# Loading the first pair of a batched matmul in two halves per operand, with its own order of k

## The chip, the cores and the metric

The kernel runs on one core of a Trainium2 chip. The metric is the device time in microseconds (us), the median over several executions. The profile's span, from the first to the last instruction, is some 2 us shorter than that time: in the profiled run of the kernel before, 121.9 us against 123.82.

Words used below: the profile counts 16 DMA engines for the core. They move data between DRAM and the on-chip memory (SBUF; a cast here reads a tile of 128 partitions, 128x2048 in the profile). A kernel issues a DMA from a queue, here that of SyncE. An engine's share of a transfer comes as packets, whose times and sizes the trace has (but not which engine moved them). In this kernel TensorE multiplies (512 matmuls), VectorE casts (32 casts), ScalarE moves results out (32 copies).

## The reference

```python
batch, m, k, n = 16, 512, 512, 512
a: (batch, k, m) float32;  b: (batch, k, n) float32

def reference(a, b):
    return np.matmul(a.transpose(0, 2, 1), b).astype(np.float32)
```

Sixteen products of 512 x 512 matrices. In all 33.55 MB are read and 16.78 MB are written.

## The kernel before

Matrices are taken in pairs (G = 2). A pair of one operand is one load of 2 MB: partition (g, q) receives R = 8 consecutive rows of matrix g, 16 KB side by side. Four input buffers take a and b of two pairs. VectorE casts each buffer in two halves (v = 0, 1) to bf16, TensorE sums over k, ScalarE evicts, and all stores are issued after all loads.

```python
G = 2; Q = P // G      # 64 partitions for each matrix of the pair
R = K // Q; V = 2; RV = R // V
in_v = [x.rearrange("(pair g) (q r) m -> pair (g q) r m", g=G, r=R) for x in (a, b)]
out_v = out.rearrange("(pair g) (c t) n -> pair c g t n", g=G, t=T)
NX = 4
# ... (tiles and semaphores)
for n in range(2 * pairs):                      # SyncE: loads
    if n >= NX:
        nc.sync.wait_ge(s_in, n - NX + 1)       # a cast has freed the buffer
    nc.sync.dma_start(x_ts[n % NX][:], in_v[n % 2][n // 2]).then_inc(s_x[n % NX], 16)
for i in range(pairs - 1):                      # SyncE: stores
    nc.sync.wait_ge(s_out, i + 1)
    nc.sync.dma_start(out_v[i], o_ts[i % NO][:]).then_inc(s_o if i else s_o0, 16)

for i in range(pairs):                          # VectorE: casts
    for v in range(V):
        # ... (waits for TensorE)
        for n in (2 * i, 2 * i + 1):
            if v == 0:
                nc.vector.wait_ge(s_x[n % NX], 16 * (n // NX + 1))
            nc.vector.tensor_copy(out=(bbf_ts if n % 2 else abf_ts)[v][:],
                                  in_=x_ts[n % NX][:, v * RV:(v + 1) * RV, :]).then_inc(s_cast, 1)
            # ... (after v == 1: s_in + 1)
```

The sum over k may be taken in any order, so long as a and b agree. That is why a pair may have its own assignment of rows to partitions.

## Time and profile before

| | before |
|---|---|
| time, median of 6 runs | 124.0 us (123.82 to 124.23) |
| span of the profiled run | 121.9 us |
| mean DMA rate, share of 16 engines' time | 413 GB/s, 97.6% |
| TensorE / VectorE / ScalarE busy | 51% / 31% / 26% |
| first cast of a, of b | 8.84 us, 13.67 us |
| last computing ends | 92.6 us |

The profile's slices are 40 equal parts of the span, each digit the busy share in tenths. The prediction below shows them, the waits and the start.

### The profile page before, as it was taken

How to read it: one execution, taken by the hardware profiler on the slowest of the kernel's cores; microseconds unless marked ns; L12 is line 12 of the kernel's file. 1: busy time of each engine (PE TensorE's matmuls, PEld its weight loads, DVE VectorE, ACT ScalarE, POOL GpSimd, SP SyncE). 2: the span in 40 equal slices, each digit the busy share in tenths (PEclk: the TensorE clock that was granted, in tenths of full speed). 3: DMA queues.
4: the chain of work that ended last, by engine and by line, in shares of the span. 5: the costliest groups of instructions: out<-in, count | busy, mean ns of one | idle time of the engine just before them, and what ended most of it. 6: DMA issues, size and time to landing. Idle time of an engine off the chain costs nothing. (4 is left out here: it accounts for less than half of the span.)

```text
span 121.9 us, 1261 instructions
## 1 busy us (share of the span) xinstructions
PE 62.5 (51%) x512; PEld 35.8 (29%) x512; DVE 38.0 (31%) x48; ACT 31.8 (26%) x41; POOL 0.2 (0%) x4
## 2 busy tenths in 40 slices
PE   0000099989669749969919988946960000000000
PEld 0000044546246314536605645624630000000000
DVE  0003560784194092474356247419000000000000
ACT  4000000480920830190470075091083000000000
POOL 0000000000000000000000000000000000000000
PEclk9999999999999977999995899999999655555555
DMA  5899999999999999999999999999999999999994
GB/s 108 360 430 430 436 430 430 430 430 430 430 430 430 430 430 436 430 430 430 430 430 430 430 430 430 436 390 428 428 430 430 430 428 430 430 430 428 428 428 175
DMA packets 4480, 50.33 MB, mean 413 GB/s; under 512 B 384, under 2 KB 384, under 8 KB 384
## 3 DMA queue, kind: packets, MB, share of 16 engines
q1 hardware_dynamic: 4480, 50.33, 97.6%
HBM read 33.55 MB, written 16.78 MB: 413 GB/s over the span
## 5 line engine op out<-in xcount | busy, mean ns | idle before, releaser
L103 PE MATMUL ps<-bbf,abf 64*128 64x512 bf16 x512 | 62.5, 403 | 27.9 <-PEq L98 27.9
L103 PEld LDWEIGHTS ps<-bbf,abf 64*128 64x128 bf16 x512 | 35.8, 114 | 54.1 <-issue 37.8
L121 ACT COPY o<-ps 128x1024 f32<-128x1024 f32 x32 | 30.1, 1026 | 59.8 <-PE ps L103 59.8
L82 DVE CAST abf<-x 128x2048 bf16<-128x2048 f32 x16 | 19.6, 1224 | 26.6 <-PE ps L103 17.6
L82 DVE CAST bbf<-x 128x2048 bf16<-128x2048 f32 x16 | 19.6, 1225 | 20.8 <-DMA x<-in_b_dram 20.8
L126 ACT ACTIVATE done<-done 1x1 uint32<-1x1 uint32 x8 | 1.6, 196 | 0.0
L121 ACT ACT_TABLE_LOAD x1 | 1.3, 1283 | 0.9 <-SPq L64 0.9
L88 DVE MEMSET done<- 1x1 f32 x16 | 0.9, 59 | 0.0
L148 POOL MEMSET const-bfloat16-1.0<- 128x1 bf16 x1 | 0.1, 101 | 0.0
L148 POOL MEMSET const-uint8-127<- 128x1 uint8 x1 | 0.1, 101 | 0.0
L148 POOL MEMSET const-float32-0.0<- 128x1 f32 x1 | 0.1, 98 | 0.2 <-issue 0.2
L148 POOL MEMSET const-float32-1.0<- 128x1 f32 x1 | 0.1, 98 | 0.0
## 6 DMA issues: line engine op xcount, KB each, us to landing
x<-in_a_dram SPq DMA_DIRECT2D x8, 2048.0 KB, 12.1
x<-in_b_dram SPq DMA_DIRECT2D x8, 2048.0 KB, 15.9
out_dram<-o SPq DMA_DIRECT2D x8, 2048.0 KB, 30.8
```

Source lines behind the costliest of these rows:

```text
L82: nc.vector.tensor_copy(out=(bbf_ts if n % 2 else abf_ts)[v][:], in_=x_ts[n % NX][:, v * RV:(v + 1) * RV, :],).then_inc(s_cast, 1)
L88: nc.vector.memset(dve_done[:, n:n + 1], 0.0).then_inc(s_in, 1)
L103: mm = nc.tensor.matmul(ps_ts[g][h][:, t % 2, :], a_m[:, t], bbf_ts[v][rows, r, :], start=(v == 0 and r == 0), stop=(v == V - 1 and r == R ...
L121: ev = nc.scalar.copy(out=o_ts[i % NO][:, g, 2 * h:2 * h + 2, :], in_=ps_ts[g][h][:])
L126: nc.scalar.memzero(act_done[:, i:i + 1]).then_inc(s_out, 1)
L148: nc = _bacc.Bacc("TRN2", target_bir_lowering=False, num_devices=1)
```

## The change

Pair 0 alone is loaded in two DMAs per operand. Each takes half of the rows of both matrices (256 of 512), as 8 KB runs that lie side by side in DRAM. All other loads stay as they were. The apparent intent is a first half that is complete in itself; but the wait asks for both halves before the first cast, so no work can begin on one half.

```diff
+    in0_v = [
+        x[0:G].rearrange("g (v q r) m -> v g q r m", v=V, r=RV) for x in (a, b)
+    ]
...
-            nc.sync.dma_start(x_ts[n % NX][:], in_v[n % 2][n // 2]).then_inc(s_x[n % NX], 16)
+            if n < 2:
+                for v in range(V):
+                    nc.sync.dma_start(
+                        x_ts[n][:, v * RV:(v + 1) * RV, :], in0_v[n][v]
+                    ).then_inc(s_x[n], 16)
+            else:
+                nc.sync.dma_start(x_ts[n % NX][:], in_v[n % 2][n // 2]).then_inc(s_x[n % NX], 16)
...
-                        nc.vector.wait_ge(s_x[n % NX], 16 * (n // NX + 1))
+                        nc.vector.wait_ge(s_x[n % NX], 16 * (n // NX + 1 + (n % NX < 2)))
```

## The prediction

> **What bounds the kernel now.** I read the overview in slices first, because it says which resource never rests.
>
> ```profile
> PE   0000099989669749969919988946960000000000
> DVE  0003560784194092474356247419000000000000
> ACT  4000000480920830190470075091083000000000
> DMA  5899999999999999999999999999999999999994
> GB/s 108 360 430 430 436 430 430 430 430 430 430 430 430 430 430 436 430 430 430 430 430 430 430 430 430 436 390 428 428 430 430 430 428 430 430 430 428 428 428 175
> DMA packets 4480, 50.33 MB, mean 413 GB/s; under 512 B 384, under 2 KB 384, under 8 KB 384
> ...
> q1 hardware_dynamic: 4480, 50.33, 97.6%
> ```
>
> TensorE, VectorE and ScalarE all have gaps and are done by slice 32 of 40. The DMA row is at 9 from the third slice to the last but one, at 428 to 436 GB/s with one dip to 390. So the kernel is bound by its 50.33 MB of traffic: 50.33 MB at 430 GB/s is 117.0 us, and the rest of the 121.9 us span is the start and the end. The packet line says more: 24 DMAs were issued (16 loads, 8 stores), and there are 384 packets under 512 B, which is 24 x 16. Every DMA left 16 small packets, one for each of 16 engines: each transfer was spread over all of them. One engine's share of the steady rate is 430 / 16 = 26.9 GB/s.
>
> Next come the chain of work that ended last and the DMA queue's own waits, to see whether anything but traffic sets the end.
>
> ```profile
> 90.68 0.92 ACTq L64
> 91.60 0.92 ACT o L121
> 92.52 0.06 ACT done L126
> ```
>
> ```profile
> SPq L68 <- DVE done L88: 59.1, 12, 13.0
> SPq L159 <- DMA out_dram<-o: 27.8, 1, 27.8
> ```
>
> The last computing ends at 92.6 us; the 27.8 us behind it are spent waiting for stores that are queued. The 59.1 us that the queue waited for VectorE before reissuing a load cost nothing: earlier loads still filled the engines. Computing has some 29 us of slack at the end.
>
> Last, the timeline of the start, which is what the change touches.
>
> ```profile
> 0.94 0.39 SPq L68 DMA_DIRECT2D x<-in_a_dram  x1
> 1.39 0.42 SPq L68 DMA_DIRECT2D x<-in_b_dram  x1
> 1.86 0.42 SPq L68 DMA_DIRECT2D x<-in_a_dram  x1
> 2.32 0.69 SPq L68 DMA_DIRECT2D x<-in_b_dram  x1
> 8.84 1.23 DVE L82 CAST abf<-x 128x2048 bf16<-128x2048 f32 x1 [8.84 <-DMA x<-in_a_dram]
> 13.67 1.23 DVE L82 CAST bbf<-x 128x2048 bf16<-128x2048 f32 x1 [3.60 <-DMA x<-in_b_dram]
> ...
> 16.08 0.33 SPq L68 DMA_DIRECT2D x<-in_a_dram  x1
> ```
>
> The four first loads are issued within 3 us. Each operand of a pair is 2 MB; b of pair 0 lands 4.8 us after a, as 2.10 MB at 430 GB/s (4.9 us) says. The first reload is issued 2.4 us after b's first cast starts.
>
> [...] Both old access patterns have 128 outermost; for the store the author even put the 128 rows ahead of g. [...]
>
> **The change part by part.**
>
> *What it seems to offer, and doesn't.* Halves of 1 MB could let casting start earlier, but VectorE's wait for pair 0 now asks for 32 on each semaphore, so the first cast still waits for both halves. Nothing in computing starts earlier. The new order of k is the same for a and b and sums the same products. Casts, matmuls and evictions keep count and shape: zero.
>
> *Two more issues.* Each is 0.39 to 0.42 us on the queue that starts transfers. Pair 1's loads are issued some 0.9 us later, while earlier loads fill the engines: zero on the path.
>
> *Smaller packets.* Pair 0 now comes in 4 x 128 = 512 packets of 8 KB instead of 256 of 16 KB. The stores already move 8 KB runs, at 428 against 430 GB/s in the late slices. On 4.19 MB (9.75 us) that is under 0.1 us.
>
> *The new outermost dimension.* This is the expensive part. The old source view merges g and q: 128 rows, 16 KB apart. In the new one a half is (g, q, r, m) with v fixed: g steps by a whole matrix (1 MB), q by 8 KB, and 64 x 8 KB is only half a matrix, so g and q cannot merge. The slowest dimension on the DRAM side is g, of size 2; on the on-chip side it is 128 partitions. [...] I therefore expect each of the four new DMAs to run on **two engines, not sixteen**, and on the same two[...].
>
> The sum for one of these two engines:
> - Before, its share of pair 0 was 4.19 MB / 16 = 0.262 MB, at 26.9 GB/s 9.75 us.
> - After, it is 4.19 MB / 2 = 2.097 MB, 78.0 us.
> - All else, 14 loads and 8 stores, stays on 16 engines, so it also carries what it carried before.
> - Added: 78.0 - 9.75 = 68.2 us, in series on this engine.
>
> How much of that is on the path? All of it. In the kernel before each engine works without a break from about 2 us to the end (DMA at 9 in each slice), so two of them get 68.2 us more and nothing gets less on them. The other fourteen run dry, which helps nobody, because a later load is only complete when its shares on the two slow engines land. Nor do these two rest: pair 0 lands at about 2 + 78 = 80 us; then pair 1's shares follow (another 9.75 us, to about 90), and the first reload is issued some 2.4 us after pair 0's last cast can start, about 83 us, well before 90. From there the picture before repeats, moved by 68 us. Sum: 124.0 + 68.2 = 192.2 us; with 0.2 for 8 KB packets and longer start effects, **192.4 us**.
>
> **The rivals.**
> 1. *All 16 engines are used anyway* (the transfer is regrouped on its way to the engines[...]). For it: nothing in the kernel's code says two engines, and the stores have a dimension of 2 too. Against it: that 2 stands second, behind 128. The change would then only swap 16 KB for 8 KB packets in 4 of 50 MB: 123.7 to 124.4 us.
> 2. *Sixteen engines and a quicker start.* The second slice moves only 360 GB/s; smaller first packets could fill the pipeline sooner. At full rate from slice 1 the first two slices would move 860 against 468, so the most to win is (860 - 468) / 430 x 3.05 = 2.8 us, and much of that is the delay before the first issue at 0.94 us. I would give it 0.5 us: 123.5 us, still within 2%.
> 3. *Two engines, but more loss than the sum*: a gap between pair 1 and the first reload[...]. That issuing can block is visible: one store's issue took 9.07 us against 0.44 for the quickest. I expect pair 1's loads to be held back this way, but they sit behind pair 0 on the two engines in any case. It could add a few us: 195 to 200.
> 4. *Two engines that go faster with the others silent.* If memory, not the engine, set the 26.9 GB/s, two alone could do better. [...] The steady 430 in both directions speaks for a limit of the engines.
>
> **Range and chances.** Rivals 3 and 4 set the range around 192.4: 186 to 199. Rivals 1 and 2 together get 0.12[...]. Faster by over 2% (under 121.5) needs more than the start can give: 0.01. Slower: 0.87.
>
> **What would show it right or wrong.**
> - Small packets: 22 x 16 + 4 x 2 = 360 with two engines, 416 with sixteen. Data packets are 4352 in both.
> - GB/s near 2 x 26.9 = 54 in the slices before 80 us, apart from what pair 1's loads add on the others; about 430 in the later stretch, at least where all engines have work.
> - The queue's share of 16 engines' time down from 97.6% to about 62% (the same work over 190 us).
> - First cast of a near 41 us (half of 78, plus 2), of b near 80; first reload near 83.
> - The first computing at 80 and the last some 68 us later than before, near 161.
> - If the two first casts stay near 9 and 14 us, the engine count was the wrong step, and the time is 124. If b is cast at 80 but the end is far from 192, the step "nothing rests after that" was wrong.

The sum: 124.0 + 68.2 + 0.2 = 192.4 us, but the two engines in it stand there as an assumption; experiments 1 and 2 test it.

## The result, and the profile after

The changed kernel takes 200.11 us (199.56 to 200.53, 6 runs) against 124.0 us. The ratio is 1.613, with a 95% interval of 1.610 to 1.616. Ratios here are the mean time of one kernel's fast runs over that of the other's fast runs of the same rounds, so not quite the ratio of the medians.

The slices of the changed kernel, each 4.97 us long, and its packets:

```profile
PE   0000000000000000006998586977698776000000
DVE  0000000020000000007272727272726360000000
ACT  2000000000000000000075252255225616000000
...
DMA  0111111111129992114999999999999999999991
GB/s 20 53 53 56 53 53 53 54 54 53 53 89 241 292 238 74 53 56 122 419 383 347 426 389 436 442 422 413 436 422 434 419 426 426 426 429 431 427 416 51
DMA packets 4712, 50.33 MB, mean 253 GB/s; under 512 B 360, under 2 KB 360, under 8 KB 360
...
q1 hardware_dynamic: 4712, 50.33, 64.2%
```

For ten slices the core moves 53 GB/s, which is 2 of 16 engines (2 x 26.9 = 54), and the DMA row stands at 1 tenth (a share of 0.13 from 4 to 58 us, and 2/16 is 0.125). The small packets are 360 and not 416: 22 DMAs left 16 of them and four left 2. Then come three slices, 59.6 to 74.5 us, in which the DMA row is at 9 but only 238 to 292 GB/s move: the engines are occupied, yet slow. From slice 20 on the rate is mostly back above 410, as before.

The timeline of issues and casts of the changed kernel answers to the one of before in the prediction:

```profile
0.96 1.26 SPq L74 DMA_DIRECT2D x<-in_a_dram  x2
2.26 37.02 SPq L74 DMA_DIRECT2D x<-in_b_dram  x2
39.32 19.21 SPq L78 DMA_DIRECT2D x<-in_a_dram  x1
42.82 1.23 DVE L92 CAST abf<-x 128x2048 bf16<-128x2048 f32 x1 [42.82 <-DMA x<-in_a_dram]
58.57 2.11 SPq L78 DMA_DIRECT2D x<-in_b_dram  x1
89.47 1.23 DVE L92 CAST bbf<-x 128x2048 bf16<-128x2048 f32 x1 [45.42 <-DMA x<-in_b_dram]
...
91.88 0.33 SPq L78 DMA_DIRECT2D x<-in_a_dram  x1
```

The columns are start, duration, engine, line and what was done. Casts of pair 0 begin at 42.8 and 89.5 us instead of 8.8 and 13.7. Look also at the durations of issuing: b's two DMAs kept SyncE for 37 us and pair 1's first load for 19 us, against 0.4 to 0.7 us before. The first of pair 1's packets starts at 59.2 us, so the other 14 engines stood idle until then. Of pair 1's 256 packets of 16 KB, 224 (14 shares of 16) started from there to 76 us and the other 32 only from 87.9 us on, when the two engines were coming to the end of pair 0.

From the first cast of b to the end there are 121.9 - 13.67 = 108.2 us before and 198.6 - 89.47 = 109.1 us after. Nearly all of the loss lies ahead of that cast.

The rates of the changed kernel in stretches of its time show what happened after 59 us (the last two columns are the DMA share and GB/s; the first is the stretch):

```profile
4.00:58.00 54.00, 0.00 (x0) 0.00 (x0) 1.23 (x1) 0.00 (x0) 0.00 (x0) 1.00 0.13 53
59.00:64.00 5.00, 0.00 (x0) 0.00 (x0) 0.00 (x0) 0.00 (x0) 0.00 (x0) 1.00 1.01 242
64.00:66.00 2.00, 0.00 (x0) 0.00 (x0) 0.00 (x0) 0.00 (x0) 0.00 (x0) 1.00 1.01 365
66.00:76.00 10.00, 0.00 (x0) 0.00 (x0) 0.00 (x0) 0.00 (x0) 0.00 (x0) 1.00 0.95 229
77.00:88.00 11.00, 0.00 (x0) 0.00 (x0) 0.00 (x0) 0.00 (x0) 0.00 (x0) 1.00 0.13 54
```

Before 59 us and after 77 us two engines work alone at 53 to 54. Between, 16 engines work (share about 1), at little more than half of 430. The trace's own packet records say the same from the other side: an 8 KB packet of the two engines takes 0.309 us when they are alone and mostly 0.5 to 0.67 us here, and a 16 KB packet of the other fourteen mostly 1.0 to 1.25 us instead of 0.611. From 67 to 75 us none of 101 such packets took less than 0.99 us, so all fourteen were slow. This is the part that the prediction lacked. The stretch from 64 to 66 us is different: there 38 of 40 such packets took 0.66 to 0.81 us and only two 1.10 and 1.29; of nine 8 KB packets six took 0.33 to 0.41 us and three 0.58 to 0.67.

### The profile page after: what moved, and what is told of

Same layout as the page of the kernel before. It is cut to its first block, busy times and chain, and to the rows that moved or that the text cites. A ratio compares the mean times of both kernels' runs of the same rounds, so it can differ in the third digit from the quotient of the medians.

```text
span 198.6 us, 1263 instructions
## 1 busy us (share of the span) xinstructions
PE 62.7 (32%) x512; PEld 35.9 (18%) x512; DVE 38.0 (19%) x48; ACT 31.8 (16%) x41; POOL 0.2 (0%) x4
## 5 line engine op out<-in xcount | busy, mean ns | idle before, releaser
L92 DVE CAST abf<-x 128x2048 bf16<-128x2048 f32 x16 | 19.6, 1224 | 61.0 <-DMA x<-in_a_dram 42.8
```

## The experiments

Seven kernels were run. The first three ask why 16 engines became two and what it is that costs; the next two what the 8 us beyond the prediction are; the last two follow up a miss of mine.

### 1. Two DMAs per operand in the old order of k

```diff
-                        x_ts[n][:, v * RV:(v + 1) * RV, :], in0_v[n][v]
+                        x_ts[n][:, v * RV:(v + 1) * RV, :],
+                        in_v[n][0][:, v * RV:(v + 1) * RV, :],
```

The source's slowest dimension is again the 128 rows; the count of DMAs, their size and the 8 KB runs are those of the change.

> Pair 0 in the same four DMAs of 8 KB runs, but in the old order of k, so that the source's slowest dimension is 128 rows and not g = 2. Theory 'two engines': all 16 engines are used again, 416 packets under 512 B, first casts near 9 and 14 us, time 124.0 (123.6 to 124.6). Rival 'smaller packets or two more issues cost the time': clearly over 126, up to 200.

Measured: correct, 124.18 us (124.07 to 124.44), ratio 1.002 (0.9997 to 1.0037). The page of this run:

```profile
DMA  3999999999999999999999999989999999999993
GB/s 72 399 428 428 444 428 428 439 428 433 428 428 444 439 428 434 434 428 428 434 434 428 428 428 428 423 337 431 423 428 428 428 428 428 428 428 428 428 428 147
DMA packets 4768, 50.33 MB, mean 411 GB/s; under 512 B 416, under 2 KB 416, under 8 KB 416
```

There are 416 small packets, so 26 DMAs of 16 shares each, and casts at 8.58 and 13.47 us. Halving the loads, 8 KB packets and two more issues cost nothing that can be told from zero. The rival falls. What remains as the cause is the source's pattern, in which two things differ: the size of the outermost dimension, and runs that lie side by side. Experiment 2 separates them.

### 2. The new order of k, one DMA per half and per matrix

```diff
                 for v in range(V):
-                    nc.sync.dma_start(
-                        x_ts[n][:, v * RV:(v + 1) * RV, :], in0_v[n][v]
-                    ).then_inc(s_x[n], 16)
+                    for g in range(G):
+                        nc.sync.dma_start(
+                            x_ts[n][g * Q:(g + 1) * Q, v * RV:(v + 1) * RV, :], in0_v[n][v][g]
+                        ).then_inc(s_x[n], 16)
```

(The wait counts four DMAs per buffer.) The bytes go where the change puts them; only g is no longer a dimension of a DMA.

> The new order of k and the 8 KB runs side by side are kept, but each of the four DMAs is cut into one per g, 64 rows each, so that g is no dimension of a DMA any more. Theory 'two engines': 16 engines again, 480 packets under 512 B, time 124 to 134 (64 rows at a time may not keep all engines at full rate), guess 127. Rival 'runs that lie side by side in DRAM are slow to read, whatever engine reads them': pair 0 still lands near 80 to 90 us, time near 200.

Measured: correct, 132.57 us median, ratio of the fast runs 1.068 (1.066 to 1.071); one further run, at 140.32, was 6% above the others of this kernel and so is a slow one. With g gone from each DMA there are 480 small packets, so 16 engines again: runs that lie side by side don't confine these DMAs to two engines (16 small packets each), and the dimension of 2 in front did (2 each in the changed kernel). But my guess of 127, inside the stated 124 to 134, was 5.6 us too low:

```profile
DMA packets 4832, 50.33 MB, mean 386 GB/s; under 512 B 480, under 2 KB 480, under 8 KB 480
...
3.00:20.00 17.00, 0.00 (x0) 0.00 (x0) 1.23 (x1) 0.00 (x0) 0.00 (x0) 1.00 1.03 223
22.00:82.00 60.00, 45.76 (x386) 27.04 (x388) 29.97 (x38) 22.89 (x30) 0.00 (x0) 0.97 1.01 432
```

While pair 0 is loaded, all engines are busy (share 1.03) at 223 GB/s, half of the 432 of the later stretch. At 223 GB/s the pair's 4.19 MB take 18.8 us instead of 9.75, so 9.1 us more; the time rose by 8.6 us (132.57 against 123.95 for the kernel before beside it). Experiments 6 and 7 ask why.

### 3. Pair 1's loads held until pair 0 has landed

```diff
+            if n == 2:
+                nc.sync.wait_ge(s_x[1], 32)
```

> The changed kernel, but pair 1's two loads are issued only when pair 0 has landed whole. Theory 'contention': the 8 us by which the two engines ran late were lost beside pair 1's traffic on the other 14; without it pair 0 lands at 2.4 + 256 x 0.309 = 81.5 us (b cast near 82 instead of 89.5), about 2 us are then lost before pair 1 starts, and the time is about 195 (193 to 197). Rival 'the two engines slow down after 58 us by themselves': b cast still near 89 us, time 201 to 204.

Measured: correct, 195.42 us (195.24 to 195.79), ratio 1.576 (1.573 to 1.580). The timeline and the windows of this run:

```profile
43.04 1.23 DVE L94 CAST abf<-x 128x2048 bf16<-128x2048 f32 x1 [43.04 <-DMA x<-in_a_dram]
82.18 0.36 SPq L80 DMA_DIRECT2D x<-in_a_dram  x1
82.19 1.23 DVE L94 CAST bbf<-x 128x2048 bf16<-128x2048 f32 x1 [37.92 <-DMA x<-in_b_dram]
```

```profile
4.00:81.00 77.00, 0.00 (x0) 0.00 (x0) 1.23 (x1) 0.00 (x0) 0.00 (x0) 1.00 0.13 54
86.00:140.00 54.00, 45.21 (x358) 25.20 (x354) 25.00 (x31) 19.08 (x25) 0.00 (x0) 0.91 1.01 432
```

With nothing beside them, the two engines keep 54 GB/s to the end and b is cast at 82.19 us, 7.3 us sooner than in the changed kernel. So the two engines do not slow down by themselves: pair 1's loads beside them cost the 7.3 us. From this cast to the end it is 193.3 - 82.2 = 111.1 us, 2.9 us more than before the change: pair 1's first packet starts only at 83.2 us, and no packet starts from 82 to 83. The cast of b (expected near 82) and the time (193 to 197) are both as expected.

### 4. Only a in the new way

```diff
-            if n < 2:
+            if n < 1:
...
-   16 * (n // NX + 1 + (n % NX < 2))
+   16 * (n // NX + 1 + (n % NX < 1))
```

> Only a of pair 0 comes in the new way, b in one DMA as before (the orders of k then differ, so pair 0's result is wrong on purpose). Theory 'two engines, and contention per load that passes on the other 14': half the extra work, 128 x 0.309 - 4.9 = 34.7 us, so 159 without contention; three loads pass instead of two, at about 3.8 us each, so about 168 (164 to 172). Rival 'the loss beside the two engines is a single fixed cost': 159 + 8 = 167 cannot be told from it, but 159 to 161 would deny contention.

Measured: 168.7 us (168.69 and 168.72), ratio 1.360 (1.357 to 1.364); the result is wrong, for the two operands' orders of k differ in pair 0. Half of the extra work on two engines accounts for 159 us; the rest, 9.7 us, is what three passing loads cost, after the 7.3 us that two cost in experiment 3. The loss beside the two engines is there again, so the case of no contention (159 to 161) is refuted. Whether it is a cost per load stays undecided: 9.7 lies between the 7.3 of a single fixed cost and the 11.0 of three loads at the 3.65 us each of experiment 3. (The expectation's own sum was off: 159 and three times 3.8 is 170.4, not 168.) The windows of this run show something else:

```profile
23.00:26.00 3.00, 0.00 (x0) 0.00 (x0) 0.00 (x0) 0.00 (x0) 0.00 (x0) 1.00 0.98 336
27.00:35.00 8.00, 0.00 (x0) 0.00 (x0) 0.00 (x0) 0.00 (x0) 0.00 (x0) 1.00 1.00 229
36.00:40.00 4.00, 0.00 (x0) 0.00 (x0) 0.00 (x0) 0.00 (x0) 0.00 (x0) 1.00 1.01 233
40.40:42.40 2.00, 0.00 (x0) 0.00 (x0) 0.00 (x0) 0.00 (x0) 0.00 (x0) 1.00 1.03 356
```

The slowness is not even. By the count of 8 KB packets in the trace, the two engines were at the first eight of the 64 rows of their half from 23.2 to 26.6 us, and reached the 32nd row at 40.4 us. In both stretches the rate is far higher than between. Where they are makes a difference; but a row stands for a place on chip and for a place in DRAM at once.

### 5. The same with the source moved by 64 KB

```diff
-        x[0:G].rearrange("g (v q r) m -> v g q r m", v=V, r=RV) for x in (a, b)
+        x.rearrange("b k m -> (b k) m")[32:32 + G * K].rearrange(
+            "(g v q r) m -> v g q r m", g=G, v=V, r=RV
+        ) for x in (a, b)
```

> As the run with a alone in the new way, but its source starts 32 rows (64 KB) further on in DRAM while the rows land in the same partitions (result wrong on purpose). In that run the loads that passed on the 14 other engines went at full rate for a short while when the two engines wrote the first 8 partitions of their halves (from 23.2 to 26.6 us) and again near the 32nd (40.4 to 42.4), and at half rate between. Theory 'the place on chip': both quick stretches stay where they are in time, 350 GB/s or more from 23 to 26 us and about 225 from 27 to 40; time 168.7. Rival 'the place in DRAM': the quick stretch moves by 8 rows, so 23 to 26 us is slow (about 225) and 36 to 40 us is quick (over 330).

Measured: 169.46 us in its one run. Its output is wrong, which doesn't matter for the time.

```profile
23.00:26.00 3.00, 0.00 (x0) 0.00 (x0) 0.00 (x0) 0.00 (x0) 0.00 (x0) 1.00 1.03 358
27.00:35.00 8.00, 0.00 (x0) 0.00 (x0) 0.00 (x0) 0.00 (x0) 0.00 (x0) 1.00 1.01 227
36.00:40.00 4.00, 0.00 (x0) 0.00 (x0) 0.00 (x0) 0.00 (x0) 0.00 (x0) 1.00 1.01 229
40.40:42.40 2.00, 0.00 (x0) 0.00 (x0) 0.00 (x0) 0.00 (x0) 0.00 (x0) 1.00 0.96 332
```

The quick stretches stayed where they were; 36 to 40 us, which the rival wanted quick, is at 229. So the addresses that the two engines read don't set the rate. What goes with it is the row of the half that they write: the partitions, by the reading taken here. In these runs row and partition number always go together, so a rule by a packet's number within its DMA is not excluded.

### 6 and 7. Half the partitions, or one stretch of DRAM?

Experiment 2's half rate could come from writing 64 partitions at a time or from reading 512 KB in one stretch. Experiment 6 reads the same stretches but writes each across 128 partitions; experiment 7 keeps 64 partitions but reads runs that are 16 KB apart.

```diff
# 6
-                            x_ts[n][g * Q:(g + 1) * Q, v * RV:(v + 1) * RV, :], in0_v[n][v][g]
+                            x_ts[n][:, 2 * (2 * v + g):2 * (2 * v + g) + 2, :],
+                            in0_v[n][v][g].rearrange("q (h s) m -> (q h) s m", s=2),
# 7
+                            x_ts[n][g * Q:(g + 1) * Q, v * RV:(v + 1) * RV, :],
+                            in_v[n][0][g * Q:(g + 1) * Q, v * RV:(v + 1) * RV, :],
```

> As the run with one DMA per half and per g, reading the same 512 KB pieces of DRAM, but each piece is spread over all 128 partitions in 4 KB runs instead of 64 partitions in 8 KB runs (data in the wrong place, result wrong on purpose). Theory 'half the partitions, half the rate': pair 0 back at about 428 GB/s, casts near 9 and 14 us, time 124.0 to 125.0. Rival 'a piece that lies in one stretch of DRAM is read at half rate': still 215 GB/s and about 132.6 us.

> Eight DMAs of 64 partitions by 8 KB as in the run with one DMA per half and per g, but in the old order of k (8 KB runs 16 KB apart in DRAM); result correct. Theory 'half the partitions, half the rate': 215 GB/s again and 132.6 us (131.5 to 133.5). Rival 'the order in DRAM': back to 124.

Measured: experiment 6 took 125.39 us in its fast run, a little over the expected range (its other run, 134.75 us, was slow, at a granted clock of 0.617, and is left out). Its output is wrong, which doesn't matter for the time. Experiment 7 is correct at 132.8 us, ratio 1.071 (1.068 to 1.073). Both lines are from the loading of pair 0, experiment 6 first (its start, up to 8 us, is left out; in 3 to 12 us it is 391 GB/s, against 224 for experiment 7):

```profile
8.00:13.00 5.00, 0.00 (x0) 0.00 (x0) 1.23 (x1) 0.00 (x0) 0.00 (x0) 1.00 1.05 428
```

```profile
3.00:20.00 17.00, 0.00 (x0) 0.00 (x0) 1.23 (x1) 0.00 (x0) 0.00 (x0) 1.00 1.01 223
```

128 partitions give 428 GB/s from the DRAM pieces of experiment 2, 64 give 223 from other ones. It is the half of the partitions that halves the rate. How it does so, no run shows.

## Why the prediction was right or wrong

**What bounds the kernel: right.** DMA traffic. No computing engine became a limit: the last computing ended at 169.3 us of 198.6.

**The halves bring no earlier start, the extra issues and the 8 KB packets cost nothing: right.** Experiment 1 has all three and stays at 124.18 us.

**Two engines: right.** 360 small packets and 53 to 54 GB/s, as written. The step from g = 2 in front to two engines, an assumption when it was written, is now seen here: the changed kernel reads the same addresses into the same places as experiment 2, but with g as the outermost dimension, and sixteen shares become two (2 small packets for each of these DMAs instead of 16). No run tries another size of g.

**The size of the extra work, 68.2 us plus 0.2: right.** Moved by 68.4 us, the first cast of b would go from 13.67 to 82.1. Where nothing interferes, in experiment 3, it starts at 82.19. The prediction also said "about 80", for 2 + 78. That count falls short by the slow start: for the kernel before, 2 + 9.75 = 11.75 is 1.9 us short of its cast at 13.67. The first cast of a came at 42.82 for the predicted 41.

**The same picture from there, only later: nearly right.** From b's cast to the end it is 109.1 us instead of 108.2. The rate dips after the reloads that are issued at 91.9 and 102.1 us: 221 GB/s from 92 to 94 us and 309 from 102 to 108. No run tests why. As b's cast came later than predicted, so did the first reload (91.88 us for about 83) and the last computing (169.3 for 161).

**Pair 1's loads are harmless: wrong, and this is the step that failed.** The sum gave the two engines 26.9 GB/s each throughout, with all else, 14 loads and 8 stores, spread over 16 engines as before. In its part on two more issues the prediction put a delay of 0.9 us on pair 1's loads and called it "zero on the path"; in its third rival it let them be held back but argued that "they sit behind pair 0 on the two engines in any case". That is true of their shares on those two engines, the 32 packets from 87.9 us on. It overlooked the other fourteen shares, which the sum treated as running beside the two at no cost to them. While they ran, from 59 to 76 us, everything dropped to 229 to 242 GB/s, apart from 365 in 64 to 66 us, and the two engines that set the end were slowed with the rest. That term was taken as 0 and measured 7.3 us (89.47 against 82.19). With the 0.9 us above it makes 8.2 of the 8.3 us by which the span of 198.6 exceeds the predicted 121.9 + 68.4 = 190.3.

**The rivals.** Sixteen engines and a quicker start are refuted by the packets. Two engines alone got no faster than 54 GB/s in 77 us of experiment 3, 27 for each, as when all sixteen run (430 / 16 = 26.9), so memory that all share does not set that rate. Whether the engine itself does, as argued, or something else, no run here separates. The third rival, more loss than the sum, is what came, but not by its gap: the two engines went from pair 0 to pair 1's shares without a gap, and no run shows a cost of the blocked issuing in itself. The top of the range, 199, was set for a gap of a few us and was too low by 1.1 us.

**What stays open.** Experiment 3 shows that the passing loads cause the loss (b's cast at 82.19 us instead of 89.47), and experiment 5 that it does not go by the addresses that the two engines read (36 to 40 us at 229 GB/s, after 233 in experiment 4). Why the stretches at the first rows and at the 32nd are quick (332 to 358 GB/s in these two runs) and those between are not (227 to 233), no run shows. What can be read is this: in the quick stretch of the changed kernel, 64 to 66 us, a few packets of either size took about twice the time of the rest (1.10 and 1.29 us against 0.66 to 0.81; 0.58 to 0.67 against 0.33 to 0.41); and in experiment 2 an 8 KB packet took about twice its 0.309 us (an estimate from that run's window: 16 engines x a share of 1.03 x 8192 bytes / 223 GB/s = 0.61 us). But in the slow stretches all fourteen were slow, with no 16 KB packet under 0.99 us from 67 to 75 us. What holds up all of them no run here shows.

## What to carry to other kernels

Before you reshape a load, write down the outermost dimension of its source as the DMA will see it. Here a small one in front, g = 2, took the transfer from 16 engines to 2 and its rate from about 430 to 53 GB/s. The count of small packets told it at once, 16 for each DMA that was spread over all and 2 for each of these. Splitting the DMA along the small dimension was only half a cure, as each piece then reached just half of the partitions (223 GB/s, 132.57 us); the order with 128 rows outermost cost nothing (124.18 us). And when you add up work on a few overloaded engines, do not take their rate as fixed while the others are moving data too: here that cost 7.3 us.
